# Reciprocal roots of the statistics: a power on GpSimd in place of ScalarE's root and VectorE's reciprocal, in a two-layer trunk

## The chip, the cores and the metric

One core of a Trainium2 chip. The metric is the device time of one execution in microseconds (us). The core has five engines that work side by side, each executing its own instructions in order and waiting by semaphores for the others: TensorE (PE; its weight loads are PEld), VectorE (DVE), ScalarE (ACT), GpSimd (POOL) and SyncE (SP), which here only issues DMAs. ScalarE evaluates its functions from tables; where the next function lies in another set, an ACT_TABLE_LOAD row stands ahead of it. GpSimd takes some operations from different libraries of code, and a switch shows in the instruction order as an extra ISA row without operands.

## The reference, cut to what matters

Two layers over 2176 tokens (2048 latent, 128 context) of width 1024. Layer 0 projects the modulated tokens to a query latent, a key/value latent, a rotary key, two gates and a pooling input, and runs latent attention beside multi-scale pooling; layer 1 is a gated MLP that mixes positions in chunks of 128. Every normalisation needs one reciprocal root for each token:

```python
def rmsnorm(x, g):
    xf = x.astype(jnp.float32)
    y = xf * lax.rsqrt(jnp.mean(xf * xf, axis=-1, keepdims=True) + EPS)
    return (y * g.astype(jnp.float32)).astype(x.dtype)
...
    q = (rmsnorm(q_lat, q_norm) @ w_uq).reshape(B, T, MLA_HEADS, QK_NOPE + QK_ROPE)
    ckv = rmsnorm(kv_lat, kv_norm)
...
    h = rmsnorm(x, norm_pre[l]) * (1 + scale) + shift
    x = x + gate * rmsnorm(out, norm_post[l])
```

## The kernel before, in words

Channels lie on the 128 partitions, tokens on the columns. The tokens go in five blocks of 512, 512, 512, 384 and 256 columns. Every product in fp32 quality is made of three TensorE products of a rounded part and a remainder (`mm3`, L175 to L179); so each weight that is loaded gets a rounded copy on ScalarE (L423) and its remainder on VectorE (L160 by way of `sub`), and each result that goes back into TensorE likewise.

A norm works in two steps. The squares are summed over the partitions, so that the sum stands in all 128 rows: with `AR_*` 0 by a product with ones on TensorE (L319, L320), with 1 by `partition_all_reduce` on GpSimd (L311). Only AR_POST is 1, which holds for the output norms of all blocks of layer 0 and of the first four of layer 1, nine in all. Then `invert` turns the row of sums so that one number per token is left on the partitions (a 32 x 32 block transpose on VectorE, L295), takes scale * x + EPS, root (ScalarE, L300) and reciprocal (VectorE, L302) of k = n / 32 columns (16, 12 or 8), and transposes back with a broadcast (L303). It is called 47 times: 30 with a scale (one for the first block's statistics in `first_stats`; five each for the kv latent and the q latent; four in `prep0`, the input norms of blocks 1 to 4; nine after a partition_all_reduce in `post`; five for layer 1's input norm, called h1 here; one in `last_post`) and 17 without, in the attention, where the reciprocal is of a softmax sum and no root is taken.

The stages, by the profile's clock: block by block the input projection, to about 510 us. Its work per block is `kv_consume` and `q_consume` (L500, L533), whose statistics, inversion, scaling (L511, L545) and casts to TensorE's two parts (L512, L548) come between two groups of matmuls; the gates' evacuations with Silu (L591); and the pooling sums on GpSimd (L633 to L650), whose results VectorE gates (L653, L655) and stores to mix_d, a transfer that releases the GpSimd buffers of the next sums. Then the attention, to about 1100 us. Then, block by block, the output projection of layer 0 (`OA`), the gated MLP (`IN`) and its output projection (`OUT`). `post` scales the results by the inverted norm (L988, one of four tiles of a block on GpSimd in layer 0), adds the residual (L992) and stores. In `IN`, `chunk_norm` (L1155 to L1160) makes its own reciprocal root, of one column, as a power with exponent -1/2 on GpSimd (L1158); the constant `mhalf` belongs to it.

The order of the instructions on each engine is not the order in the source: a scheduler lays out the whole program at build time, and the buffers of each pool set what may run ahead. The weights are loaded ahead in a queue; the parts of weight m are made when TensorE has freed those of weight m-3, so two whole weights are in hand.

Of the kernel before, what the change touches and what calls it, by code (L numbers as in the profile page):

```python
# [11 lines left out]
AF = mybir.ActivationFunctionType  # L12
ALU = mybir.AluOpType

P = 128
# [6 lines left out]
EPS = 1e-6  # L22
# [91 lines left out]
def trunk_kernel(ctx, tc, xT, cols_in, cond_in, ident_in, edge_in, rope_in, w_ada, w_ada_T, w_in_t, w_inp_T, w_pool,  # L114
# [32 lines left out]
    def st():  # L147
        return spool.tile([P, 32], F32, tag="s", name=nm("s"))
# [13 lines left out]
    V, S, G, PE = nc.vector, nc.scalar, nc.gpsimd, nc.tensor  # L162
# [29 lines left out]
    eps = const.tile([P, 1], F32, name="eps")  # L192
    V.memset(eps, EPS)
    mhalf = const.tile([P, 1], F32, name="mhalf")
# [98 lines left out]
    def invert(src, r, n, scale=None):  # L293

        V.transpose(r[:, 1, :n], src)  # L295
        c = st()
        k = n // 32
        col = r[:, 1, :n].rearrange("p (k c) -> p k c", c=32)[:, :, 0]
        if scale is not None:
            S.activation(out=c[:, :k], in_=col, func=AF.Sqrt, bias=eps[:, 0:1], scale=scale)  # L300
            col = c[:, :k]
        V.reciprocal(out=c[:, :k], in_=col)  # L302
        V.transpose(r[:, 1, :n].rearrange("p (k c) -> p k c", c=32), c[:, :k, None].broadcast_to([P, k, 32]))  # L303
        return r[:, 1, :n]

# [8 lines left out]
    def rstd(r, n, d, pool, tag):  # L314

        if pool:
            return invert(r[:, 0, :n], r, n, 1.0 / d)
        ps = ps1(tag)
        PE.matmul(ps[:, :n], ones[1], r[:, 0, :n], start=True, stop=False)  # L319
        PE.matmul(ps[:, :n], ones[1], r[:, 1, :n], start=False, stop=True)  # L320
        return invert(ps[:, :n], et(), n, 1.0 / d)
# [596 lines left out]
    def finish(b):  # L918

        den = ps1("D")  # L920
        PE.matmul(den, ones[1], b.hl[:, 0], start=True, stop=False)
        PE.matmul(den, ones[1], b.hl[:, 1], start=False, stop=True)
        oh = et()
        S.copy(oh[:, 0], b.o)
        rd = invert(den[:, :QB], et(), QB)
        gt = b.gt
        yield
        g.gated = G.tensor_tensor(out=gt[:, 1], in0=gt[:, 0], in1=rd, op=ALU.mult)
        out = ps1("D")
        for h in ([b.h] if b.h is not None else range(H)):  # L930
            c = slice(0, QB) if b.h is not None else slice(h * P, (h + 1) * P)
            PE.matmul(out[:, c], Wuv[:, h], oh[:, 0, c], start=True, stop=True)
        yield
        mx = oh[:, 1]
        V.tensor_tensor(out=mx, in0=out, in1=gt[:, 1], op=ALU.mult)
        if b.h is not None:
            store(ST_MX, mix_d[b.h, :, b.t0:b.t0 + QB], mx)
        else:
            dma(mix_d[0:4, :, DEC:T].rearrange("h p n -> p h n"), mx.rearrange("p (h n) -> p h n", h=H))
# [328 lines left out]
    for i in range(len(steps) + LAG + PV_BEHIND + 2):  # L1268
        if 0 <= i - LAG < len(steps):
            step_exp(*steps[i - LAG])  # L1270
        k = i + 1 - LAG
# [12 lines left out]
        k = i - MAX_AT  # L1284
# [142 lines left out]
```

## Time and profile before

| | |
|---|---|
| time, median of 3 runs | 2087.75 us (2087.69 to 2091.03) |
| the profiled execution | 2087.39 us, its span 2085.6 us |
| mean granted TensorE clock | 0.989 of full speed |
| TensorE busy | 2001.2 us, 96% of the span |
| VectorE busy | 1469.1 us, 70% |
| ScalarE busy | 1098.6 us, 53% |
| GpSimd busy | 580.7 us, 28%, two thirds of it in the attention |

The span is the time from the first to the last instruction that the profiler records; the execution's own time is 1.8 us more. Busy shares are means over stages with different limits. TensorE is busy nearly all the time, so the profile is to be read from its waits.

### The profile page before, as it was taken

How to read it: one execution, taken by the hardware profiler on the slowest of the kernel's cores; microseconds unless marked ns; L12 is line 12 of the kernel's file. 1: busy time of each engine (PE TensorE's matmuls, PEld its weight loads, DVE VectorE, ACT ScalarE, POOL GpSimd, SP SyncE). 2: the span in 40 equal slices, each digit the busy share in tenths (PEclk: the TensorE clock that was granted, in tenths of full speed). 3: DMA queues.
4: the chain of work that ended last, by engine and by line, in shares of the span. 5: the costliest groups of instructions: out<-in, count | busy, mean ns of one | idle time of the engine just before them, and what ended most of it. 6: DMA issues, size and time to landing. Idle time of an engine off the chain costs nothing.

```text
span 2085.6 us, 26154 instructions
## 1 busy us (share of the span) xinstructions
PE 2001.2 (96%) x9652; PEld 1666.0 (80%) x9652; DVE 1469.1 (70%) x2222; ACT 1098.6 (53%) x1285; POOL 580.7 (28%) x405
## 2 busy tenths in 40 slices
PE   6898999999999999999989999999999999999997
PEld 3787777998777777777758788888888888889997
DVE  4688977665887878878784898455665556477575
ACT  4634444544676767667664545443355335445555
POOL 1003020111478686868771120001101100010000
PEclk9999999999999999999999999999999999999999
DMA  9577767676111011101124564334524542364463
GB/s 355 191 259 244 242 226 233 211 227 191 45 31 47 30 46 31 46 30 33 49 86 162 174 210 147 116 131 162 172 83 141 190 142 101 122 224 160 129 222 126
DMA packets 123696, 300.62 MB, mean 144 GB/s; under 512 B 12144, under 2 KB 39088, under 8 KB 123568
## 3 DMA queue, kind: packets, MB, share of 16 engines
q1 hardware_dynamic: 105168, 258.58, 37.3%
q10 hardware_dynamic: 13728, 23.60, 3.7%
q0 software_dynamic: 4672, 16.78, 2.3%
q8 instruction: 76, 1.25, 0.2%
q14 instruction: 52, 0.43, 0.1%
HBM read 243.23 MB, written 55.67 MB: 143 GB/s over the span
## 4 chain that ended last, share of the span: by engine, by line
PE 66%; DVE 12%; POOL 7%; issue 5%; ACT 4%; DMA 3%; SPq 0%; DVEq 0%; POOLq 0%; ACTq 0%
PE psA L178 18%; PE psA L179 18%; PE psA L177 18%; POOL e L886 4%; DVE h L865 3%; POOL w L873 2%; DVE run L845 2%; DVE w L160 2%; PE psB L915 1%; ACT h L835 1%; PE psA L820 1%; PE psA L821 1%; PE psA L824 1%; PE psA L823 1%; PE psA L822 1%
## 5 line engine op out<-in xcount | busy, mean ns | idle before, releaser
L177 PE MATMUL psA<-h,w 128*128 128x512 f32 (+2 forms) x1600 | 575.7, 360 | 9.1 <-ACT e L591 6.6
L179 PE MATMUL psA<-h,w 128*128 128x512 f32 (+2 forms) x1600 | 573.2, 359 | 0.2 <-DVE w L160 0.2
L160 DVE TENSOR_TENSOR w<-r,w 128x1024 fp32r<-128x1024 f32 x280 | 349.2, 1250 | 291.4 <-PE psA L178 214.0
L178 PE MATMUL psA<-h,w 128*128 128x512 f32 (+2 forms) x1536 | 548.8, 357 | 2.0 <-DVE h L160 2.0
L423 ACT CAST w<-r 128x1024 fp32r<-128x1024 f32 x280 | 292.0, 1049 | 240.5 <-PE psA L179 189.2
L177 PEld LDWEIGHTS psA<-h,w 128*128 128x128 f32 x1600 | 302.9, 189 | 49.8 <-ACT e L591 7.3
L179 PEld LDWEIGHTS psA<-h,w 128*128 128x128 f32 x1600 | 302.8, 189 | 38.3 <-DVE w L160 0.4
L178 PEld LDWEIGHTS psA<-h,w 128*128 128x128 f32 x1536 | 290.9, 189 | 38.4 <-DVE h L160 3.1
L873 POOL TENSOR_TENSOR w<-h,w 128x1024 fp32r<-128x1024 f32 x105 | 252.1, 2402 | 132.4 <-ACT w L871 130.5
L845 DVE TENSOR_TENSOR run<-psA,run 128x512 f32<-128x512 f32 x240 | 163.4, 681 | 15.2 <-ACT h L835 14.5
L867 ACT ACTIVATE h<-h 128x1024 f32<-128x1024 f32 (+1 forms) x145 | 143.7, 1014 | 53.1 <-DVE h L865 52.9
L865 DVE TENSOR_TENSOR h<-h,psC 128x1024 f32<-128x1024 f32 (+1 forms) x145 | 163.5, 1145 | 0.9 <-PE psC L859 0.9
L835 ACT COPY h<-psA 128x1024 f32<-128x1024 f32 (+1 forms) x145 | 138.3, 964 | 34.1 <-PE psA L824 33.8
L178 PE MATMUL psA<-o,w 128*128 128x512 f32 (+2 forms) x368 | 134.0, 366 | 0.0
L886 POOL TENSOR_TENSOR e<-e,h 128x512 f32<-128x512 f32 x92 | 120.2, 1307 | 5.8 <-ACT h L867 2.2
L871 ACT CAST w<-h 128x1024 fp32r<-128x1024 f32 x105 | 110.5, 1054 | 11.0 <-PE psB L179 10.9
L639 POOL TENSOR_TENSOR pl<-pl 128x527 f32<-128x527 f32 (+2 forms) x16 | 22.0, 1374 | 329.4 <-PE psA L179 118.9
L179 PE MATMUL psA<-o,w 128*128 128x512 f32 (+2 forms) x304 | 109.1, 361 | 0.0
L177 PE MATMUL psA<-o,w 128*128 128x512 f32 (+2 forms) x304 | 108.9, 361 | 0.0
L177 PE MATMUL psA<-w,h 128*128 128x512 f32 x272 | 106.7, 393 | 1.2 <-ACT o L1147 1.2
L178 PE MATMUL psA<-w,h 128*128 128x512 f32 x272 | 106.1, 390 | 0.1
L179 PE MATMUL psA<-w,h 128*128 128x512 f32 x272 | 105.8, 390 | 0.0
(297 smaller groups left out, 3559.7 us busy)
## 6 DMA issues: line engine op xcount, KB each, us to landing
r<-in_w_inc_t_dram SPq DMA_DIRECT2D x80, 512.0 KB, 3.5
r<-in_w_in_t_dram SPq DMA_DIRECT2D x60, 512.0 KB, 4.1
r<-in_w_oap_t_dram SPq DMA_DIRECT2D x40, 512.0 KB, 3.4
r<-in_w_incv_t_dram SPq DMA_DIRECT2D x40, 512.0 KB, 4.1
r<-in_w_outc_t_dram SPq DMA_DIRECT2D x40, 512.0 KB, 3.5
r<-in_w_ada_T_dram SPq DMA_DIRECT2D x32, 512.0 KB, 4.5
r<-wp_d SPq DMA_DIRECT2D x20, 512.0 KB, 5.9
h<-in_w_ada_dram SPq DMA_DIRECT2D x16, 512.0 KB, 10.5
```

What stands on the lines that cost most here:

```text
L160: eng.tensor_tensor(out=out, in0=a, in1=f(hi), op=ALU.subtract)
L177: PE.matmul(ps, w[0], x[0], start=first, stop=False)
L178: PE.matmul(ps, w[0], x[1], start=False, stop=False)
L179: PE.matmul(ps, w[1], x[0], start=False, stop=last)
L423: S.copy(hi, raw)
L835: S.copy(s[:, :nt], ps[:, :nt])
L845: V.tensor_tensor(out=b.max, in0=ps[:, a], in1=s[:, 0] if p == 0 else b.max, op=ALU.max)
L865: V.tensor_tensor(out=s[:, :nt], in0=s[:, :nt], in1=b.m[:, None, :].broadcast_to([P, nt, QB]), op=ALU.subtract)
L867: S.activation(out=s[:, :nt], in_=s[:, :nt], func=AF.Exp, scale=SM_SCALE)
L871: S.copy(ph[:, :nt], s[:, :nt])
L873: low = behind(G.tensor_tensor(out=pl[:, :nt], in0=s[:, :nt], in1=f(ph[:, :nt]), op=ALU.subtract), g.gated)
L886: behind(G.tensor_tensor(out=b.pool[:, 0], in0=b.pool[:, 0], in1=s[:, a], op=ALU.add), low or g.gated)
```

## The change

In `invert`, where a scale is given, ScalarE's root and VectorE's reciprocal are replaced: VectorE computes scale * x + EPS in one instruction, and GpSimd raises the result to the power -1/2. Without a scale the reciprocal stays. From L302 on, lines of the kernel after are one higher (L303 becomes L304, L591 L592).

```diff
--- before.py
+++ after.py
@@ -297,9 +297,10 @@
         k = n // 32
         col = r[:, 1, :n].rearrange("p (k c) -> p k c", c=32)[:, :, 0]
         if scale is not None:
-            S.activation(out=c[:, :k], in_=col, func=AF.Sqrt, bias=eps[:, 0:1], scale=scale)
-            col = c[:, :k]
-        V.reciprocal(out=c[:, :k], in_=col)
+            V.tensor_scalar(out=c[:, :k], in0=col, scalar1=scale, scalar2=EPS, op0=ALU.mult, op1=ALU.add)
+            G.tensor_tensor(out=c[:, :k], in0=c[:, :k], in1=mhalf.broadcast_to([P, k]), op=ALU.pow)
+        else:
+            V.reciprocal(out=c[:, :k], in_=col)
         V.transpose(r[:, 1, :n].rearrange("p (k c) -> p k c", c=32), c[:, :k, None].broadcast_to([P, k, 32]))
         return r[:, 1, :n]
```

The scheduler lays the program out anew. ScalarE has 43 ACT_TABLE_LOAD rows after, 69 before: the 18 at L300 go, and 8 others that had brought another table back after a root. On VectorE 30 RECIPROCAL rows become 30 TENSOR_SCALAR rows. GpSimd gets 30 powers, and behind the start 18 library switches where there were 12.

GpSimd in block 1 of the input projection, before; `pl` are the pooling buffers, one MEMSET per channel group:

```order
L648 TENSOR_TENSOR pl_1530<-pl_1530,edge 128x8
L633 MEMSET pl_1651 128x8
L639 TENSOR_TENSOR pl_1653<-pl_1651 128x519
L643 TENSOR_TENSOR pl_1654<-pl_1653 128x517
L643 TENSOR_TENSOR pl_1653<-pl_1654 128x513
L643 TENSOR_TENSOR pl_1654<-pl_1653 128x505
L648 TENSOR_TENSOR pl_1654<-pl_1654,edge 128x8
```

The same place after; s_1400 is the kv latent's inversion, s_1506 the q latent's:

```order
L649 TENSOR_TENSOR pl_1530<-pl_1530,edge 128x8
L634 MEMSET pl_1651 128x8
L301 TENSOR_TENSOR s_1400<-s_1400,mhalf 128x16
L640 TENSOR_TENSOR pl_1653<-pl_1651 128x519
L644 TENSOR_TENSOR pl_1654<-pl_1653 128x517
L644 TENSOR_TENSOR pl_1653<-pl_1654 128x513
L644 TENSOR_TENSOR pl_1654<-pl_1653 128x505
L301 TENSOR_TENSOR s_1506<-s_1506,mhalf 128x16
L649 TENSOR_TENSOR pl_1654<-pl_1654,edge 128x8
```

The kv power stands between a group's MEMSET and its first sum, the q power behind the group's last sum (L644, before it L643) and ahead of the edge product.

GpSimd around the last partition_all_reduce (L311, after it L312; its first ISA row is the library switch), before. The DMA rows store layer 1's results of block 3:

```order
L311 ISA
L311 ISA e_15571<-e_15319 128x384
L167 DMA out_dram<-o_15317 128x2x384
L167 DMA out_dram<-o_15396 128x2x384
L1158 ISA
L1158 TENSOR_TENSOR s_15703<-s_15703,mhalf 128x1
L1158 TENSOR_TENSOR s_15711<-s_15711,mhalf 128x1
L167 DMA out_dram<-o_15462 128x2x384
```

And after:

```order
L312 ISA
L312 ISA e_15571<-e_15319 128x384
L301 ISA
L301 TENSOR_TENSOR s_15610<-s_15610,mhalf 128x12
L167 DMA out_dram<-o_15317 128x2x384
L167 DMA out_dram<-o_15396 128x2x384
L1159 TENSOR_TENSOR s_15703<-s_15703,mhalf 128x1
L1159 TENSOR_TENSOR s_15711<-s_15711,mhalf 128x1
L167 DMA out_dram<-o_15462 128x2x384
```

The switch back, an ISA row at L1158 behind two stores before, now stands directly behind the reduce, for the power of 12 columns.

VectorE at the same place, before; s_15610 is this inversion, the L160 rows with `w` make weight remainders:

```order
L295 STREAM_TRANSPOSE e_15571<-e_15571 128x384
L160 TENSOR_TENSOR w_15577<-r_15573,w_15575 128x1024
L302 RECIPROCAL s_15610<-s_15610 128x12
L303 STREAM_TRANSPOSE e_15571<-s_15610 128x384
L988 TENSOR_TENSOR o_15317<-o_15317,e_15571 128x2x384
L160 TENSOR_TENSOR w_15595<-r_15591,w_15593 128x1024
L988 TENSOR_TENSOR o_15396<-o_15396,e_15571 128x2x384
L988 TENSOR_TENSOR o_15462<-o_15462,e_15571 128x2x384
L160 TENSOR_TENSOR w_15621<-r_15617,w_15619 128x1024
```

And after:

```order
L295 STREAM_TRANSPOSE e_15571<-e_15571 128x384
L300 TENSOR_SCALAR s_15610<-e_15571 128x12
L160 TENSOR_TENSOR w_15577<-r_15573,w_15575 128x1024
L160 TENSOR_TENSOR w_15595<-r_15591,w_15593 128x1024
L304 STREAM_TRANSPOSE e_15571<-s_15610 128x384
L160 TENSOR_TENSOR w_15621<-r_15617,w_15619 128x1024
L989 TENSOR_TENSOR o_15317<-o_15317,e_15571 128x2x384
L989 TENSOR_TENSOR o_15396<-o_15396,e_15571 128x2x384
L1156 BN_STATS s_15703<-o_15614 128x6
```

The first half of the inversion is one row now, two weights' remainders follow it, and the second transpose (L304) stands behind them and ahead of the others; block 3's scaling (L989) comes behind it.

## Rows read from the trace of the kernel before

**Rows 1.** The page, part 1: busy time and share of the span
```profile
PE 2001.2 (96%) x9652; PEld 1666.0 (80%) x9652; DVE 1469.1 (70%) x2222; ACT 1098.6 (53%) x1285; POOL 580.7 (28%) x405
```

**Rows 2.** TensorE's waits (line, releaser: us in total, times, longest us)
```profile
PE psA L177 <- ACT e L548: 7.8, 2, 5.9
PE psA L177 <- ACT e L591: 6.6, 3, 3.7
...
PE psB L1171 <- DVE o L1160: 2.2, 1, 2.2
```

**Rows 3.** Groups by line (xcount | busy us, mean ns | idle before, releasers)
```profile
L300 ACT ACT_TABLE_LOAD x18 | 23.1, 1283 | 0.3
...
L302 DVE RECIPROCAL s<-s 128x16 f32<-128x16 f32 (+2 forms) x30 | 7.0, 234 | 9.1 <-ACT s L300 9.1
...
L886 POOL TENSOR_TENSOR e<-e,h 128x512 f32<-128x512 f32 x92 | 120.2, 1307 | 5.8 <-ACT h L867 2.2
...
L1158 POOL TENSOR_TENSOR s<-s,mhalf 128x1 f32<-128x1 f32 x17 | 9.9, 591 | 88.7 <-DVE s L1157 80.3 <-issue 8.4
...
L650 POOL TENSOR_TENSOR e<-e,edge 128x8 f32<-128x8 f32 x8 | 1.6, 203 | 0.3
```

**Rows 4.** Timeline of ScalarE, block 0 (start us, us, instruction)
```profile
102.53 1.28 ACT L591 ACT_TABLE_LOAD   x1
103.82 1.03 ACT L591 ACTIVATE e<-psA 128x1024 f32<-128x1024 f32 x1
```

**Rows 5.** Timeline of GpSimd, block 1 (in brackets the idle time before, releaser)
```profile
192.47 0.11 POOL L633 MEMSET pl<- 128x8 f32 x1
...
198.73 4.65 POOL L643 TENSOR_TENSOR pl<-pl 128x517 f32<-128x517 f32 x3 [1.77 <-DMA mix_d<-pl]
```

**Rows 6.** Timeline of VectorE, block 1
```profile
193.29 0.74 DVE L655 SCALAR_TENSOR_TENSOR pl<-pl,cols,pl 128x504 f32<-128x504 f32 x1
...
205.70 0.69 DVE L303 STREAM_TRANSPOSE e<-s 128x512 f32<-128x512 f32 x1
```

**Rows 7.** Timeline of VectorE, blocks 2 and 3
```profile
307.06 0.71 DVE L295 STREAM_TRANSPOSE e<-psD 128x512 f32<-128x512 f32 x1
...
310.10 0.70 DVE L303 STREAM_TRANSPOSE e<-s 128x512 f32<-128x512 f32 x1
...
395.19 0.58 DVE L295 STREAM_TRANSPOSE e<-psD 128x384 f32<-128x384 f32 x1
...
397.05 0.58 DVE L303 STREAM_TRANSPOSE e<-s 128x384 f32<-128x384 f32 x1
...
401.81 0.59 DVE L295 STREAM_TRANSPOSE e<-psD 128x384 f32<-128x384 f32 x1
...
403.22 0.58 DVE L303 STREAM_TRANSPOSE e<-s 128x384 f32<-128x384 f32 x1
```

**Rows 8.** Timeline of GpSimd, second half
```profile
1155.89 3.36 POOL L988 TENSOR_TENSOR h<-h,e 128x1024 f32<-128x1024 f32 x1 [8.23 <-DVE e L303]
...
1434.49 2.39 POOL L988 TENSOR_TENSOR o<-o,e 128x1024 f32<-128x1024 f32 x1 [7.34 <-DVE w L160]
...
1978.13 3.31 POOL L311 PARTITION_ALL_REDUCE e<-e  x1 [70.47 <-DVE e L975]
...
2005.92 1.21 POOL L1158 TENSOR_TENSOR s<-s,mhalf 128x1 f32<-128x1 f32 x2 [8.38 <-issue]
```

**Rows 9.** Timeline of VectorE, around 1988
```profile
1987.70 1.22 DVE L160 TENSOR_TENSOR w<-r,w 128x1024 fp32r<-128x1024 f32 x1
```

**Rows 10.** Timeline of TensorE, around 1978
```profile
1977.84 0.39 PE L179 MATMUL psA<-w,h 128*128 128x512 f32 x1
1978.07 0.39 PE L177 MATMUL psA<-w,h 128*128 128x512 f32 x1
```

**Rows 11.** Timeline of VectorE, the last inversion
```profile
2074.65 0.45 DVE L295 STREAM_TRANSPOSE e<-psC 128x256 f32<-128x256 f32 x1 [0.27 <-PE psC L1019]
...
2075.71 0.45 DVE L303 STREAM_TRANSPOSE e<-s 128x256 f32<-128x256 f32 x1
```

## The prediction

> **What bounds the kernel now.** I read the page first. TensorE is busy for 2001.2 us, 96% of the span [rows 1]: a change on the three other engines counts only where TensorE waits for them, and at the two ends. So the second view is the list of TensorE's waits [rows 2]. The inversions are behind three kinds: the casts of the q latent (L548, 7.8 us in two waits, the longest 5.9), which stand behind two inversions of a block; the evacuations at L591 (6.6 us in three), with ScalarE's function tables loaded just ahead of them; and one wait for chunk_norm's scaling (L1171, 2.2), which waits for a power on GpSimd. Third, the instructions that the change removes, and the only power that the trace has [rows 3]; then the timelines around those waits [rows 4 to 7] and around a partition_all_reduce [rows 8, 9], and the last inversion [rows 11].
>
> **What is removed.** 30 roots, 30 reciprocals (7.0 us of VectorE), and 26 of ScalarE's 69 table loads (the 18 at L300 and 8 that had to bring another table back): 26 x 1.283 = 33.4 us of ScalarE [rows 3]. Nearly all of that lies beside matmuls. What shows is the wait at L591, where a load stands straight ahead of the awaited evacuation, as at 102.53 [rows 4]: it has three waits, the longest 3.7, 6.6 in all [rows 2]. Two give back a load of 1.28 each and the third, 0.9 long, itself: **term A = -3.4** (bounds 0, if something else is late there, and -6.6, the whole wait). The Trainium skill (ScalarE: Activation LUTs, "What ACT_TABLE_LOAD costs") adds a drain of about 1380 ns to each load, 2.66 us in all. The trace does not show it: the load at 102.53 lasts 1.28, and the ACTIVATE starts at 103.82, 0.01 behind it. By the page A would be at most -5.5 (2.66, what is left of the second wait, 2.0, and 0.9), and the sum below 2 us lower.
>
> **What is added.** A VectorE tensor_scalar on the shape of the removed reciprocal (0.20 to 0.25 us, so nothing changes there), and a power on GpSimd of 16, 12 or 8 columns. Call p the time of the 16-column one. The trace has only one-column powers, 0.59 us [rows 3]. Below: further columns cost what they cost a GpSimd product, (1.307 - 0.203)/504 = 2.2 ns, so p = 0.59 + 15 x 0.0022 = 0.62. Above: all by which the power exceeds the 8-column product, 0.59 - 0.20 = 0.39, is paid for each column, so p = 0.2 + 16 x 0.39 = 6.4. No row is between; I take the geometric middle, p = 2.0 (a line through 0.59 gives 1.6 for 12 columns and 1.25 for 8), and keep both ends. Everything below is in p, because the price decides the sign.
>
> **A bare inversion: the tail.** Transpose starts at 2074.65 and ends at 2075.10, the second one starts at 2075.71 [rows 11]: root, reciprocal and hand-overs take 0.61. After: tensor_scalar 0.25 with its hand-over, then the power and 0.04. Nothing else is in flight: **term H = p8 - 0.32**, +0.9 (0.3 to +3.0).
>
> **Input projection, block 1.** Here the power shares GpSimd with the pooling sums. The new order has kv's power behind the MEMSET, which ends at 192.6 [rows 5], so the transpose L304 can start at 192.65 + p, and L656, behind it, 0.7 later: 193.35 + p, against L655's 193.29 [rows 6]. L656 matters because its DMA to mix_d is what the next GpSimd sums wait for (198.73, 4.65 long [rows 5]), and q's power stands behind those sums. They end at 203.4 + p, the power at 203.4 + 2p, and q's transpose, at 205.70 before [rows 6], starts at 203.5 + 2p. The cast that TensorE waits 5.9 us for follows: **term B = 2p - 2.2**, +1.8 (-1.0 to +10.6).
>
> **Blocks 2 and 3.** In block 2 GpSimd is idle and VectorE has other work between the two transposes of q: 307.06 to 310.10 [rows 7]. The power is ready at about 308.1 + p: **term C = 0** up to p = 2, +4.4 at 6.4. Block 3 has less between them: 395.19 to 397.05 for kv, 401.81 to 403.22 for q [rows 7]. With 0.58 for a transpose, 0.3 for the tensor_scalar and 0.15 to get on with it, the second transposes come p12 - 0.8 and p12 - 0.4 later, and the q chain is waited for soon after: **term D = 2 p12 - 1.2**, +2.0 (0 to +8.6). Block 0's kv and q, the prep inversions and the first statistics lie under other waits; if that cover were gone, each would cost at most its own p - 0.3.
>
> **Library loads.** GpSimd needs another library for partition_all_reduce than for products and powers, and loads it each way. The load is no row of its own but the idle time ahead of the first other instruction. From the reduce's end to the first product at 1155.89 that is 8.2 us; 7.3 at 1434.49; and 8.4 at 2005.92, where the row names "issue", that is, nothing else was late [rows 8]. In the kernel before the load is done only when the next product is due; the root and reciprocal don't wait for it. Now the power does, the second transpose waits for the power, and VectorE, which executes in order, holds the weight subtractions (L160) behind it. The Trainium skill (GPSIMD Engine Reference, 2.1) counts about 6 us for the first call into a new library; the rows are 1.3 to 2.4 us longer, and by the page the places below would be late by that much less, the sum about 1 us lower.
> At the first place, 1148, root and reciprocal were late anyway: the product at 1155.89 waited for the transpose L303, so this started not before 1155 [rows 8]. Now it starts between 1155 + p and 1156.5 + p, and GpSimd's own product only p late; some 20 us on, TensorE waits for this chain. I take **term E = +1.5** (0 to +9, the upper end with the h1 inversion at 1178, on an idle GpSimd).
> At seven further places VectorE stands behind such a power, by my count up to 9 us (the load behind the reduce at 1418 is done at 1434.49 [rows 8], some 8 us after the reciprocal ran). TensorE has two weights in hand then, each 24 matmuls at one per 0.227 us [rows 10] with 512 columns, 5.5 us, or 18, 4.1 us, with 384, and the first weight held back is due after them: **term F = 0**; if that cover were one weight, three places would cost some 3.5 us each (rival below).
> The last place, 1978.13, is tight: with 256 columns a weight is 12 matmuls, 2.7 us. Reduce done at 1981.44 [rows 8], library 7.3 to 8.4, power of 12 columns 1.6, transpose 0.6: w_15621's subtraction, at 1987.70 before [rows 9], starts at 1990.9 to 1992.0, some 3.2 to 4.3 late, and has two weights less its own 1.2, 4.3, to spare. VectorE has work without a break behind it, so lateness adds up: +1.5 (+0.7 to +4.9). Against it, the library load at 2005.92, for which chunk_norm's power waits 8.38 us and TensorE 2.2 [rows 2, 8], is gone, because the inversion has loaded it earlier: **term G = -0.7** (-1.5 to +2.7).
>
> **Sum at p = 2.0:** A -3.4, B +1.8, C 0, D +2.0, E +1.5, F 0, G -0.7, H +0.9 = +2.1 us. The profiled execution took 2087.39 (span 2085.6 and 1.8 around it), 0.4 below the median of 2087.75, so 2089.5. At p = 0.62 the terms give -3.4 - 1.0 + 0 + 0 + 0 + 0 - 1.5 + 0.3 = -5.6, 2081.8; at p = 6.4, -3.4 + 10.6 + 4.4 + 8.6 + 9 + 0 + 2.7 + 3.0 = +34.9, 2122.
>
> **Rivals.**
> *The power is cheap* (p below 1.2): the chains shorten, and what remains is ScalarE's relief. 2081.8 by the terms, 2078.6 if all three L591 waits go; about 2081. For it: a product's further columns are nearly free. The Trainium skill's account of GpSimd's loop (GPSIMD Engine Reference, 3.1), some 2.6 cycles per element of a tensor_tensor after a fixed part, would give this case. Against: 0.39 us above the product must be spent on something, and with one column the trace cannot tell a fixed part from a price per column.
> *The power is dear* (p above 3): it decides at kv and q in blocks 1 and 3, where both inversions of a block are in series ahead of a wait. At p = 4.4 the terms stand between +2.1 and +34.9, about +20: 2108.
> *The library loads show.* If VectorE's stall behind a power after a reduce outlasts TensorE's weights in hand, at 1418, 1633 and 1840, where GpSimd's store issues, which wait for VectorE's results, delay the load too, each costs what is over: 3 x 3.5 on top of 2089 gives 2100. It decides from a lateness of two weights, 8 to 11 us; I count up to 9. For it: 9 of the 30 powers stand straight behind a reduce. Against: no wait of [rows 2] names such a place now.
> *It does nothing*: everything is under cover but A and the tail, and the two cancel; that is inside my forecast's own range.
>
> **How the numbers follow.** Forecast, p between 1.2 and 3 and the loads covered: chance 0.42, 2089, own range 2083 to 2098. Cheap: 0.25. Dear: 0.22, 2098 to 2122. Library: 0.11. This measurement tells 0.2%, 4.2 us, from no change. Faster by that: most of the cheap case and a fifth of the forecast's, 0.30; slower: dear, library and a fifth of the forecast's, 0.41; between: 0.29. The range from 2079 to 2113 leaves out the dearest powers and little below.
>
> **What would show it.** The L301 rows on GpSimd give p at once, and whether 12 and 8 columns lie on a line. No table load ahead of L592 in blocks 0, 3 and 4; TensorE's wait for L549 longer or shorter by 2p - 2.2 in block 1; a library load behind every reduce, VectorE standing at L304 after it with TensorE not waiting, except near 1990; no wait at L1172; the last transpose p8 - 0.32 later. I am wrong if p is outside 1.2 to 3, or if TensorE waits for L160 near 1430, 1645 or 1862. A scheduler laid the whole order out anew, and a wait that it moved to a place of its own is in no term.

## The result, and the profile after

The changed kernel takes 2125.7 us (median of 5 runs, 2123.5 to 2128.6) against 2088.3 for the kernel before (5 runs): the ratio is 1.0176, with a 95% interval of 1.0161 to 1.0191. That is 37 us more, outside my range, on the side to which I had given 0.41.

The page of the changed kernel, part 1, against [rows 1]: TensorE has 5.8 us more of work, ScalarE 42 less, GpSimd 80 more.

```profile
PE 2007.0 (95%) x9652; PEld 1667.4 (79%) x9652; DVE 1471.4 (69%) x2222; ACT 1056.1 (50%) x1229; POOL 661.1 (31%) x435
```

The power's price, groups by line (count | busy us, mean ns | idle before):

```profile
L301 POOL TENSOR_TENSOR s<-s,mhalf 128x16 f32<-128x16 f32 x18 | 54.3, 3019 | 164.4 <-DVE s L300 109.0 <-issue 31.7 <-DMA h<-in_w_ada_dram 16.0
...
L301 POOL TENSOR_TENSOR s<-s,mhalf 128x12 f32<-128x12 f32 x6 | 15.3, 2543 | 57.7 <-DVE s L300 41.5 <-issue 16.1
...
L301 POOL TENSOR_TENSOR s<-s,mhalf 128x8 f32<-128x8 f32 x6 | 9.9, 1656 | 97.3 <-DVE s L300 88.6 <-issue 8.7
L1159 POOL TENSOR_TENSOR s<-s,mhalf 128x1 f32<-128x1 f32 x17 | 9.7, 580 | 71.5 <-DVE s L1158 71.5
```

The 16-column power has p = 2.9 us (the mean of 3.02 holds a few longer ones, see the last section), inside my bounds of 0.62 and 6.4 and 1 us above the value that I took. One column is 0.58, before 0.59 [rows 3].

TensorE's waits after (those of before in [rows 2]): the q latent's cast is waited for in four blocks, not two, 18.5 us in place of 7.8; the wait for ScalarE's evacuation at L592 shrank by 1.6 us only; the wait at L1172 did not go but grew to 3.0.

```profile
PE psA L177 <- ACT e L549: 18.5, 4, 7.1
...
PE psA L177 <- ACT e L592: 5.0, 4, 2.8
...
PE psA L178 <- DVE w L160: 4.4, 4, 1.7
...
PE psB L1172 <- DVE o L1161: 3.0, 1, 3.0
```

And VectorE's wait in the list of its waits, at the second transpose (L304), which in the kernel before waited for nothing (there VectorE waited 9.1 us for the roots, at the reciprocal [rows 3]): 28 of the 30 places, 88.6 us.

```profile
DVE e L304 <- POOL s L301: 88.6, 28, 7.9
```

Where the time went is read by following the same matmuls through both traces. In the kernel before:

```profile
104.90 0.50 PE L177 MATMUL psA<-h,w 128*128 128x512 f32 x1 [3.71 <-ACT e L591]
...
209.50 0.80 PE L177 MATMUL psA<-e,wch 128*128 128x512 f32 x1 [5.91 <-ACT e L548]
210.76 0.80 PE L178 MATMUL psA<-e,wch 128*128 128x512 f32 x1 [0.46 <-DVE e L160]
...
316.69 0.79 PE L178 MATMUL psA<-e,wch 128*128 128x512 f32 x1 [2.76 <-DVE e L160]
...
407.69 0.44 PE L178 MATMUL psA<-e,wch 128*128 128x384 f32 x1 [1.30 <-DVE e L160]
...
1070.56 0.50 PE L178 MATMUL psB<-w,Vh 128*128 128x512 f32 x1 [2.64 <-POOL w L873]
...
1852.03 0.50 PE L177 MATMUL psA<-w,h 128*128 128x512 f32 x1 [0.43 <-ACT o L1147]
...
1869.08 0.44 PE L177 MATMUL psA<-h,w 128*128 128x384 f32 x1 [0.43 <-ACT o L1147]
```

The same matmuls in the changed kernel:

```profile
111.19 0.80 PE L177 MATMUL psA<-h,w 128*128 128x512 f32 x1 [2.85 <-ACT e L592]
...
219.43 0.80 PE L177 MATMUL psA<-e,wch 128*128 128x512 f32 x1 [7.13 <-ACT e L549]
221.84 0.80 PE L178 MATMUL psA<-e,wch 128*128 128x512 f32 x1 [1.61 <-DVE e L160]
...
333.41 0.80 PE L178 MATMUL psA<-e,wch 128*128 128x512 f32 x1 [0.47 <-DVE e L160]
...
428.46 0.69 PE L178 MATMUL psA<-e,wch 128*128 128x384 f32 x1 [0.64 <-DVE e L160]
...
1092.12 0.50 PE L178 MATMUL psB<-w,Vh 128*128 128x512 f32 x1 [2.58 <-POOL w L874]
...
1883.33 0.50 PE L177 MATMUL psA<-w,h 128*128 128x512 f32 x1 [0.43 <-ACT o L1148]
...
1902.15 0.44 PE L177 MATMUL psA<-h,w 128*128 128x384 f32 x1 [0.43 <-ACT o L1148]
```

The one at 111.19 stood at 104.90 before: it waits for the evacuation behind the load in [rows 4]. Its lag is 6.3 us. The q latent is waited for twice in a row, for its cast (L177) and then for its remainder (L178), and only behind the second is the lag of a block settled: 11.1 after block 1 (9.9 at the cast), 16.7 after block 2, 20.8 at this place in block 3, 21.6 at the end of the attention, 31.3 at 1852, 33.1 at 1869; the last inversion's first transpose lags 35.1 (2109.71 against 2074.65 [rows 11]) and the end 36.5. The windows ahead of the attention and behind it, before and then after, say what the lag is made of (TensorE's busy us stand behind the length; PEclk is its granted clock):

```profile
0.00:505.00 505.00, 461.73 (x2313) 388.71 (x2314) 362.15 (x640) 237.27 (x320) 65.82 (x64) 0.97 0.72 241
...
1100.00:2085.60 985.60, 969.33 (x4930) 841.54 (x4928) 629.62 (x912) 465.67 (x527) 93.56 (x75) 0.99 0.46 153
```

```profile
0.00:527.00 527.00, 467.04 (x2315) 391.45 (x2316) 361.82 (x642) 213.99 (x291) 104.42 (x79) 0.96 0.69 231
...
1122.00:2122.10 1000.10, 971.11 (x4929) 840.57 (x4927) 632.98 (x912) 446.44 (x500) 135.61 (x90) 0.99 0.46 151
```

In the input projection it is 22 us: TensorE idles 60.0 in place of 43.3 us, and the same matmuls take 5.3 us more. The attention between them, where nothing changed, takes 595 us in both. Behind the attention it is 14.5: 12.7 of idleness, 1.8 of work.

### The profile page after: what moved, and what is told of

It is laid out like the page before. It is cut to its first block, busy times and chain, and to the rows that moved or that the text cites. A ratio compares the mean times of both kernels' runs of the same rounds, so it can differ in the third digit from the quotient of the medians.

```text
span 2122.1 us, 26130 instructions
## 1 busy us (share of the span) xinstructions
PE 2007.0 (95%) x9652; PEld 1667.4 (79%) x9652; DVE 1471.4 (69%) x2222; ACT 1056.1 (50%) x1229; POOL 661.1 (31%) x435
## 5 line engine op out<-in xcount | busy, mean ns | idle before, releaser
L177 PE MATMUL psA<-h,w 128*128 128x512 f32 (+2 forms) x1600 | 576.8, 361 | 12.0 <-ACT e L592 5.0
L178 PE MATMUL psA<-h,w 128*128 128x512 f32 (+2 forms) x1536 | 549.1, 358 | 2.5 <-DVE h L160 2.5
L160 DVE TENSOR_TENSOR w<-r,w 128x1024 fp32r<-128x1024 f32 x280 | 352.1, 1262 | 253.3 <-PE psA L178 175.2
L177 PEld LDWEIGHTS psA<-h,w 128*128 128x128 f32 x1600 | 303.3, 190 | 53.4 <-ACT e L592 6.5
L178 PEld LDWEIGHTS psA<-h,w 128*128 128x128 f32 x1536 | 291.1, 190 | 39.3 <-DVE h L160 3.9
L301 POOL TENSOR_TENSOR s<-s,mhalf 128x16 f32<-128x16 f32 (+2 forms) x30 | 79.5, 2651 | 319.3 <-DVE s L300 239.1
L178 PE MATMUL psA<-o,w 128*128 128x512 f32 (+2 forms) x368 | 134.0, 366 | 0.0
L872 ACT CAST w<-h 128x1024 fp32r<-128x1024 f32 x105 | 110.7, 1055 | 11.1 <-PE psB L179 10.9
L178 PE MATMUL psA<-w,h 128*128 128x512 f32 x272 | 106.5, 392 | 4.4 <-DVE w L160 4.4
L177 PE MATMUL psA<-w,h 128*128 128x512 f32 x272 | 106.5, 392 | 3.3 <-ACT h L362 1.7
L177 PE MATMUL psA<-o,w 128*128 128x512 f32 (+2 forms) x304 | 108.9, 361 | 0.0
```

The costliest lines, as they stand in the source:

```text
L160: eng.tensor_tensor(out=out, in0=a, in1=f(hi), op=ALU.subtract)
L177: PE.matmul(ps, w[0], x[0], start=first, stop=False)
L178: PE.matmul(ps, w[0], x[1], start=False, stop=False)
L872: S.copy(ph[:, :nt], s[:, :nt])
```

## The experiments

Two theories stood against each other. Theory 1: VectorE waits for the power, whose price per column is what counts. Theory 2: GpSimd is the wrong place whatever the power costs, because of hand-overs and library loads.

**One column.** The power of the first column only, broadcast by the second transpose; TensorE, ScalarE and GpSimd have the changed kernel's order of instructions, VectorE nearly so.

```diff
-            G.tensor_tensor(out=c[:, :k], in0=c[:, :k], in1=mhalf.broadcast_to([P, k]), op=ALU.pow)
+            G.tensor_tensor(out=c[:, 0:1], in0=c[:, 0:1], in1=mhalf, op=ALU.pow)
...
+            V.transpose(..., c[:, 0:1, None].broadcast_to([P, k, 32]))
```

> The changed kernel with each of the 30 powers taken of one column only, which the second transpose then broadcasts over all of the block's columns (the other columns' roots are left out, so a token gets the root of the first token of its group of partitions). Instruction order as in the changed kernel; only the power is 0.58 us in place of 2.9, 2.3 or 1.7. Theory 1, the price per column (0.16 us a column, VectorE standing at the second transpose meanwhile) is what made it slower: about 2086, from my sum at a cheap power (2081.8) plus what the library loads cost in the second half (some 5). Theory 2, GpSimd as a place (hand-overs, library loads behind every reduce) is what made it slower whatever the power costs: above 2110.

Measured: 2091.1, 1.0016 (1.0007 to 1.0026) of the kernel before, which took 2087.3 in these runs. The price of the further columns makes some 34 of the 37 us. VectorE's wait at the second transpose, in the list of its waits:

```profile
DVE e L302 <- POOL s L301: 37.6, 26, 5.7
```

51.0 us less of waiting than in the changed kernel is worth 34.6 us of time.

**Root and reciprocal behind the reduces, and the opposite.** The condition in `invert` is given to one kind of call (`pool` is true behind a partition_all_reduce); the second kernel has `not pool`.

```diff
+        if scale is not None and pool:
+            S.activation(out=c[:, :k], in_=col, func=AF.Sqrt, bias=eps[:, 0:1], scale=scale)
+            V.reciprocal(out=c[:, :k], in_=c[:, :k])
-        if scale is not None:
+        elif scale is not None:
```

> Root and reciprocal as before at the nine inversions behind a partition_all_reduce, the power at the other 21. By the windows of the two traces the changed kernel loses about 22 us up to the attention, where there is no reduce, and 14 behind it. Theory 1: the 22 stay, the 14 shrink to the tail's 1.4 and something for the h1 inversions: 2111 to 2114. Theory 2: most of the loss goes with the library loads: below 2100.

> The power only at the nine inversions behind a partition_all_reduce, root and reciprocal at the other 21. If the two parts add up: 2088 + 12 = 2100 (97 to 103). Theory 2: above 2108. If the library loads are covered, as my term F had it, and only the first and last place cost (my terms E and G at a power of 2.9 us: +3.5 and +1): 2092.

Measured: 2116.4 (1.0135, 1.0115 to 1.0155) with roots behind the reduces, 2100.8 (1.0060, 1.0037 to 1.0084) with powers only there. The 21 powers without a reduce cost 29 us, the nine behind one 13.5; together 43, some 5 more than the change as a whole. Why the parts don't add up is open; the table loads are not the reason, since the two kernels have 50 and 63 of the 69, 25 fewer together, where the change has 26 fewer. Most of the loss is not at library loads. The nine are not covered, though: they would stand at 2091 to 2092 if my term F, and E and G at p = 2.9, had held.

**No root at all.** The same place with a ScalarE function that needs no table of its own, nothing on GpSimd.

```diff
-            S.activation(out=c[:, :k], in_=col, func=AF.Sqrt, bias=eps[:, 0:1], scale=scale)
+            S.activation(out=c[:, :k], in_=col, func=AF.Identity, bias=eps[:, 0:1], scale=scale)
```

> The kernel before with ScalarE computing scale * x + EPS without the root in the same place (the root is left out), a function that lies in every table set, so that the 26 table loads are gone and nothing is put on GpSimd; the scheduler orders VectorE and ScalarE anew. It measures what the removal alone can give. My term A: -3.4 us, 2084 to 2085 (bounds 0 and -6.6). Rival, the loads are all under cover: 2088. By 33 us less on ScalarE, were it on the path: 2055.

Measured: 2081.6, 0.9971 (0.9957 to 0.9985). 43 table loads are left, as in the changed kernel. The removal alone gives 6 us (3 to 9), a little more than term A; 33 us less on ScalarE are not 33 of time.

**Powers that nobody waits for.** Same powers at the same size on GpSimd, into spare columns, while the second transpose takes a reciprocal; VectorE and ScalarE have a new order.

```diff
-            G.tensor_tensor(out=c[:, :k], in0=c[:, :k], in1=mhalf.broadcast_to([P, k]), op=ALU.pow)
+            G.tensor_tensor(out=c[:, 16:16 + k], in0=c[:, :k], in1=mhalf.broadcast_to([P, k]), op=ALU.pow)
+            d = st()
+            V.reciprocal(out=d[:, :k], in_=c[:, :k])
+            c = d
```

> The changed kernel with every power of full size still done on GpSimd, but nothing waits for it: the second transpose takes a VectorE reciprocal of the same sums instead (the root is left out of what the kernel computes). GpSimd has the same powers, library loads and places in its queue, ScalarE has no root. Theory 1, the loss is VectorE standing at the second transpose for the power (88.6 us in the changed kernel, 37.6 with a one-column power): nothing of it is left, 2081 to 2086, as without roots at all (2081.6). Rival, GpSimd's own time is what costs (pooling sums queued behind powers, products behind library loads, a port shared with VectorE): above 2095.

Measured: 2082.7, 0.9979 (0.9969 to 0.9989), against 2088.9 for the kernel before in these runs. With 82 us of powers on GpSimd and every library load, the kernel isn't told apart from the one without roots (0.9971, the intervals overlap): GpSimd's time and its queue cost nothing that shows here, the waiting for it everything. Theory 2 falls as far as GpSimd's own time goes.

**Twice the power.**

```diff
+            G.tensor_tensor(out=c[:, 16:16 + k], in0=c[:, :k], in1=mhalf.broadcast_to([P, k]), op=ALU.pow)
             G.tensor_tensor(out=c[:, :k], in0=c[:, :k], in1=mhalf.broadcast_to([P, k]), op=ALU.pow)
```

> The changed kernel with each power done twice (the first into spare columns), so that an inversion waits 5.8, 4.6 or 3.3 us of GpSimd. Between the one-column power and the full one the time grew by 34.6 us for 2.07 us more per power in the mean, 16.7 a us. Theory 1, the wait is on the path: again as steep, or steeper because less is covered: 2.65 us more, 2125 + 44 = 2170 (2160 to 2185). If by contrast only my terms' places counted (2 in block 1, 2 in block 3, one at the reduces' ends and one at the tail, some 7 to 8 a us): 2145.

Measured: 2184.8 (1.0463, 1.0448 to 1.0478): 59 us more than the changed kernel, 22 a us of power, steeper than the 16.7 below it. VectorE waits 164.3 us at the second transpose:

```profile
DVE e L305 <- POOL s L302: 164.3, 29, 11.7
```

**The price by size.** A row of powers and products in block 0, read by nobody.

```diff
+            probe = const.tile([P, 4, 64], F32, name="probe")
+            V.tensor_copy(out=probe[:, 0], in_=r[:, 0:64])
+            for k in (1, 2, 4, 8, 12, 16, 32, 64):
+                for i in range(2):
+                    G.tensor_tensor(out=probe[:, 1 + i, :k], in0=probe[:, 0, :k], in1=mhalf.broadcast_to([P, k]), op=ALU.pow)
+                G.tensor_tensor(out=probe[:, 3, :k], in0=probe[:, 0, :k], in1=mhalf.broadcast_to([P, k]), op=ALU.mult)
```

> The kernel before with a row of powers of 1, 2, 4, 8, 12, 16, 32 and 64 columns on GpSimd in block 0 (each twice, and a product of the same size behind it), into a tile that nothing reads. From the changed kernel's rows of 1, 8, 12 and 16 columns (0.58, 1.65, 2.3, 2.92) a fixed part of 0.40 and 0.158 us a column: 0.72 for 2, 1.03 for 4, 5.5 for 32, 10.5 for 64. Rival: a price in steps of a block of columns, seen as equal times for neighbouring sizes. The product: 0.2 us, nearly flat. The kernel's own time says nothing here.

Measured, timeline of GpSimd (x2 is both powers together; L515 the power, L516 the product):

```profile
86.22 3.23 POOL L515 TENSOR_TENSOR probe<-probe,mhalf 128x8 f32<-128x8 f32 x2
89.42 0.20 POOL L516 TENSOR_TENSOR probe<-probe,mhalf 128x8 f32<-128x8 f32 x1
...
94.20 6.80 POOL L515 TENSOR_TENSOR probe<-probe,mhalf 128x16 f32<-128x16 f32 x2
...
112.91 21.01 POOL L515 TENSOR_TENSOR probe<-probe,mhalf 128x64 f32<-128x64 f32 x2
```

64 columns are 10.5 us each, 8 are 1.62, 4 are 1.00: 0.159 a column on a fixed part of 0.35 (0.39 by the one-column power of 0.55), and no steps. The pair of 16 is longer than this for a reason of its own (last section). A product of 8 columns is 0.20. So of the 0.39 us by which a one-column power exceeds a small product, 0.16 is paid for the column and the rest once, which one size could not tell. The Trainium skill (GPSIMD Engine Reference, 4.1) gives elementwise work to VectorE, GpSimd being about two times slower at two-input operations (it names add, multiply and maximum, not a power); the rows are harder on this one, 1.65 us for 8 columns against some 0.2 for VectorE's reciprocal [rows 3].

**One column, not behind a reduce.** The first two edits together.

```diff
+        if scale is not None and pool:
+            S.activation(...)
+            V.reciprocal(out=c[:, :k], in_=c[:, :k])
...
+            G.tensor_tensor(out=c[:, 0:1], in0=c[:, 0:1], in1=mhalf, op=ALU.pow)
```

> The power of one column only (broadcast over the block's columns, the other columns' roots left out) at the 21 inversions that don't stand behind a partition_all_reduce, root and reciprocal as before at the nine that do. The one-column kernel took 3.3 us more than the kernel before, where a kernel in which nothing waits for a power takes 6.2 less, so waiting for cheap powers still costs some 9.5. Theory: most of that is the library load that the power waits for behind each reduce (the changed kernel lost 9.3 by having its powers there): 2082 to 2086 against 2088. Rival: it is spread over the hand-overs to GpSimd and back at all 30 places: 2088 to 2091.

Measured: 2087.8, 1.0006 (0.9993 to 1.0019), not told apart from the kernel before, and just at the rival's edge. The one-column kernel with all 30 powers stands at 1.0016, 2 us above, and the two intervals together allow -1 to 5 for the library loads. (The 9.5 is the difference of a ratio and of two medians; by the ratios alone it is 7.7, by the medians alone 10.0.) How the rest divides between hand-overs and the table loads that the nine roots bring back (50 in place of 43) stays open.

**The second transpose later.** `invert` returns its second half as a function, and the kv, q and prep inversions call it one step of the schedule later: `yield` between the power and the transpose. The last lines finish such steps at the end of a block.

```diff
-        r = rstd(hl, n, 128, AR_KV, "D")
+        r = rstd(hl, n, 128, AR_KV, "D", True)
+        yield
+        r = r()
...
+        for c in hold:
+            drain(c)
```

> The changed kernel with the second transposes of the kv, q and prep inversions written one step of the schedule later than the powers (the same operations, all of them), so that other VectorE instructions stand between, up to four where there were none to two. The power and the chain's length stay. If VectorE's standing is what costs in the input projection: most of its 22 us come back, 2105 to 2112. If the longer chain (transpose, power, transpose, scaling, cast) is what costs, it gets longer still by the step: 2125 or more.

> The same with root and reciprocal at the nine inversions behind a partition_all_reduce, where the changed kernel loses 9 us. If the first reading holds, 2096 to 2103, which isn't faster than the kernel before; by the second, 2116 or more.

Measured: 2122.7 (1.0166, 1.0146 to 1.0186), 3 us less than the changed kernel, and 2111.0 (1.0109, 1.0086 to 1.0132), 5 less than with roots behind the reduces; by the intervals neither gain is certain. Neither reading has it. The lists of waits of the first of the two kernels, VectorE's and then TensorE's:

```profile
DVE e L305 <- POOL s L301: 75.8, 25, 7.7
```

```profile
PE psA L178 <- DVE e L160: 15.1, 4, 8.6
```

VectorE stands 12.8 us less. TensorE's wait for the q latent's cast (now L557) has all but gone, 1.4 of 18.5, but it waits 15.1 for the link behind it, the remainder that VectorE makes from the same latent, the longest 8.6 in block 1. There VectorE no longer stands for q's power (q's second transpose starts at 208.61), but it stands 2.17 us for the next inversion's, ahead of q's scaling (L554), and the remainder stands behind 9.5 us of other VectorE work that the new order put ahead of it:

```profile
211.48 0.71 DVE L305 STREAM_TRANSPOSE e<-s 128x512 f32<-128x512 f32 x1 [2.17 <-POOL s L301]
212.11 1.37 DVE L554 SCALAR_TENSOR_TENSOR e<-e,cols,e 128x512 f32<-128x512 f32 x2
...
223.03 1.22 DVE L160 TENSOR_TENSOR e<-e,e 128x1024 fp32r<-128x1024 f32 x1
```

So the edit moved more than the transposes, and the run can't part the standing from the length of the chain.

**The library loaded early.** The kernel before with one small product on GpSimd behind the last reduce.

```diff
         hl = total(acc[:, 0, :n], n, ar)
+        if l == 1 and bi == NB - 2:
+            G.tensor_tensor(out=st()[:, 0:1], in0=hl[:, 0, 0:1], in1=mhalf, op=ALU.mult)
```

> The kernel before, roots and reciprocals kept, with one more GpSimd product of one column straight behind the last partition_all_reduce (it reads the reduce's result and nothing reads it), so that the other library is loaded there and not when chunk_norm's power is due. My term G had the 2.2 us wait of TensorE at L1171 as the price of that load: -2.2, 2085 against 2087.3. Rival: the wait is due to VectorE's order anyway (in the changed kernel, where the library is there in time, TensorE still waits 3.0 there): no difference.

Measured: 2084.5, 0.9979 (0.9968 to 0.9991), 4.4 us (1.9 to 6.7) where 2.2 was expected: faster than both kernels, and TensorE no longer waits at that place. Timeline of GpSimd, against [rows 8]: the load stands behind the reduce (7.00 us that "issue" ends), and chunk_norm's powers wait 1.83 us for VectorE in place of 8.38 for the load.

```profile
1990.77 0.51 POOL L979 TENSOR_TENSOR s<-e,mhalf 128x1 f32<-128x1 f32 x1 [7.00 <-issue]
...
2001.68 1.21 POOL L1160 TENSOR_TENSOR s<-s,mhalf 128x1 f32<-128x1 f32 x2 [1.83 <-DVE s L1159]
```

## Why the prediction was wrong, step by step

My sum was +2.1. At the measured p = 2.9 the same terms give +8.8, 2096 (A -3.4, B +3.6, C +0.9, D +3.4, E +3.0, F 0, G 0, H +1.3), against 2123.9 for the profiled execution of the changed kernel (span 2122.1 and 1.8). So the price of the power, which I had expected to decide, explains 7 us of the miss, and 28 lie in terms whose form was wrong. By the lags above, against these terms: 7.6 too little in block 0, 1.2 in block 1, 4.7 in block 2, 3.5 in blocks 3 and 4, 6.7 at E, 1.8 at F and 2.0 at G.

**Right.** H: the last pair of transposes has one power between them, and nothing else; timeline of VectorE after, against [rows 11]:

```profile
2109.71 0.45 DVE L295 STREAM_TRANSPOSE e<-psC 128x256 f32<-128x256 f32 x1 [0.27 <-PE psC L1020]
...
2112.16 0.45 DVE L304 STREAM_TRANSPOSE e<-s 128x256 f32<-128x256 f32 x1 [1.79 <-POOL s L301]
```

From the first one's end to the second's start it is 2.00 us in place of 0.61: +1.39, p8 - 0.32 with the p8 of 1.66 gives 1.34. B, as far as it went: with the 6.4 us by which block 1 starts late (its first transpose stands at 196.26, before at 189.82), the second transposes were to start at 192.65 + 2.9 + 6.4 = 201.95 and 203.5 + 5.8 + 6.4 = 215.7; they start at 201.97 and 215.65 (rows below), and at the cast the lag grows by the 3.6 of 2p - 2.2. The wait for the remainder behind it, which B leaves out, adds 1.2 (1.61 in place of 0.46). Where I had followed the new order of both engines instruction by instruction, the sum holds within a few tenths. D does not belong here: at its place block 3 has added 4.0, and D less a table load was to give 2.1.

**The step that failed first: "Block 0's kv and q, the prep inversions ... lie under other waits", and term C, "VectorE has other work between the two transposes".** Block 0 was to gain 1.3 and lost 6.3; block 2 was to lose 0.9 and lost 5.6. Timeline of VectorE after, second transposes of blocks 0 to 2; in brackets the time that VectorE stood for the power:

```profile
83.33 0.71 DVE L304 STREAM_TRANSPOSE e<-s 128x512 f32<-128x512 f32 x1 [3.02 <-POOL s L301]
...
94.34 0.71 DVE L304 STREAM_TRANSPOSE e<-s 128x512 f32<-128x512 f32 x1 [3.01 <-POOL s L301]
...
102.70 0.71 DVE L304 STREAM_TRANSPOSE e<-s 128x512 f32<-128x512 f32 x1 [3.01 <-POOL s L301]
...
201.97 0.71 DVE L304 STREAM_TRANSPOSE e<-s 128x512 f32<-128x512 f32 x1 [2.19 <-POOL s L301]
...
215.65 0.71 DVE L304 STREAM_TRANSPOSE e<-s 128x512 f32<-128x512 f32 x1 [2.73 <-POOL s L301]
...
328.34 0.71 DVE L304 STREAM_TRANSPOSE e<-s 128x512 f32<-128x512 f32 x1 [2.72 <-POOL s L301]
```

I read the work between the transposes from the trace of before ([rows 7]: 307.06 to 310.10) and kept it for after. But the scheduler put the second transpose right behind the power, with little or nothing between, and VectorE executes in order: for 2 to 3 us it does nothing at all, and the scalings, casts and weights behind it are late by that. In block 0 it stands 9 us so (three times 3.0), and TensorE is 6.3 late at its end. The price that I named for a lost cover, "at most its own p - 0.3" a place, comes to 7.8 for these three and would have covered it, but it stood in no term. The wait of TensorE that grew most there, from 0.81 to 2.89, is not for VectorE itself but for a weight transfer:

```profile
104.59 2.04 PE L702 MATMUL psB<-pl,e 128*128 128x128 f32 x8 [2.89 <-DMA e<-in_w_inp_T_dram]
```

SyncE issues this transfer at 100.40 in place of 95.43, in the new order behind a store (99.99) of what ScalarE copies (L703, 98.89) once VectorE's L160 of 97.63 lets it; that L160 stands behind the first two of these waits, and comes 3.5 us later than before (94.18). A cover that VectorE itself would have to provide is none while VectorE stands. That it is the waiting at this transpose is shown by "Powers that nobody waits for": the same powers, the same library loads, no wait, and the loss is gone. Which part of a wait costs, VectorE's standing or the chain that ends later, isn't parted by that, nor by "The second transpose later". Over the runs the wait at the second transpose goes with the time: 0, 37.6, 88.6 and 164.3 us of it with 2083, 2091, 2126 and 2185.

**The added waits also cost clock.** In the input projection 5.3 of the 22 us are the same matmuls taking longer: 467.0 us of TensorE at a granted clock of 0.96, against 461.7 at 0.97 before (windows above) and 458.7 at 0.98 in the one-column kernel. Windows of the changed kernel behind the waits of 2.89 (block 0, above) and 5.78 (q's cast in block 2, at 332.15):

```profile
104.59:108.34 3.75, 3.75 (x16) 3.45 (x16) 3.75 (x6) 2.05 (x3) 0.00 (x0) 0.50 0.41 140
332.10:336.10 4.00, 3.48 (x7) 2.44 (x8) 3.06 (x7) 2.45 (x3) 1.50 (x1) 0.51 0.69 234
```

The one-column kernel: the whole projection, then behind its waits of 1.82 and 2.44 at the same matmuls:

```profile
0.00:503.50 503.50, 458.65 (x2313) 386.16 (x2314) 360.81 (x641) 214.52 (x291) 72.31 (x79) 0.98 0.72 242
101.18:103.18 2.00, 2.00 (x10) 2.00 (x11) 2.00 (x4) 0.86 (x2) 0.00 (x0) 0.57 0.03 10
313.60:317.60 4.00, 3.18 (x13) 2.40 (x14) 3.60 (x10) 2.47 (x4) 1.48 (x2) 1.00 0.70 234
```

A granted clock of 0.50 is 1.2 of 2.4 GHz. In block 2 it is down behind the long wait and not behind the short one; in block 0 it is down in both kernels, so the length of the wait just ahead does not alone say it. I priced each wait at its length; the trace of before has the sign of it, matmuls of 0.80 us behind its 5.91 us wait, which I did not use.

**E was too small, F nearly right, G had the wrong sign.** From the attention's end to 1852 the lag grows by 9.7; I had 3.0 at this p. The first power did start when I said (1155 to 1156.5 and 21.6 is 1176.6 to 1178.1; it started at 1177.14), but three inversions follow each other there and VectorE stands at each second transpose, 0.8, 3.0 and 4.3 us: the lags add up. Behind the next five reduces F holds: VectorE stands up to 7.9 us there, and nothing is added up to 1852. At 1840 it fails by 1.8: TensorE waits 1.4 for L160 near 1862, on the clock of before, which the prediction had named as a sign of being wrong. The last reduce, VectorE after:

```profile
2024.43 0.58 DVE L304 STREAM_TRANSPOSE e<-s 128x384 f32<-128x384 f32 x1 [6.80 <-POOL s L301]
...
2039.75 0.14 DVE L1158 TENSOR_SCALAR s<-s 128x1 f32<-128x1 f32 x1
```

It stands 6.80 us for load and power; weights reach TensorE 1.7 us late (1 of the waits L178 <- L160 above). The library was there in time for chunk_norm's power, as I said; yet that power waited for VectorE, whose L1158 came at 2039.75, and TensorE waited 3.0 where it had waited 2.2: the lag grows by 2.0 over this stage. The gain that I booked is real, and "The library loaded early" has it, but not with an inversion standing in VectorE's way.

**A was about right in size** (6 us, 3 to 9, in the kernel without roots), and got eaten: the evacuation at 111.19 has no table load ahead of it and comes 6.3 us later, because its matmuls do. Of the rivals, the library loads, to which I gave 0.11, are part of the loss: 13.5 us at most, by the kernel with powers only there. The dear power did not come, since 2.9 lies inside my forecast's own case, just under its end of 3; what was wrong is what a microsecond of power costs. My terms had 40.5 us between p = 0.62 and 6.4, 7 a us; the runs have 16.7 a us between one column and all, and 22 above.

Open: how the loss divides between VectorE's standing and the longer chain, since the chain runs on VectorE on both sides of the power and no run changes the one alone; and how the 8 to 10 us that waiting for one-column powers costs divide.

## What to carry to other kernels

Before an operation moves to another engine, count the instructions that stand behind the one that waits for it, on an engine that executes in order: a small operation of 3 us in 30 places cost 37 us on TensorE, though that engine never touches it. Price the operation at its real size, since one column tells a fixed part from a part per column no better than one point tells a line. And read the new order around every place, not only around those where TensorE waits now: the two places that were followed so, the tail and block 1's first wait, came out within a few tenths, those that took their cover from the old trace did not.

## What the runs showed of the hardware that was not expected

A power on GpSimd that starts while a VectorE instruction is running can last longer by about what is left of that instruction. In the row of sizes (above) the first 16-column power started at 94.20, 0.03 behind the start of a VectorE L160 of 1.23 us; the pair took 6.80 us, where twice 2.9 would be 5.8, and in the changed kernel one such power took 3.81 (at 223.17, 0.16 behind the start of an L160 of 1.21). Not every instruction does that: the second 16-column power of that row started at 98.11 with 0.44 us of a transpose left and took 2.89. VectorE instructions that start while a power is running did not lengthen it: in the kernel where nobody waits VectorE worked through most of them, and the median of the 16-column power was 2.94 us in place of 2.93, with a longest of 3.82 (an L160 was running at its start). The row of the L160, timeline of VectorE in the kernel with the row of sizes:

```profile
94.17 1.23 DVE L160 TENSOR_TENSOR w<-r,w 128x1024 fp32r<-128x1024 f32 x1 [2.23 <-issue]
```
